# Conditioning matmuls in bursts of four tiles in the first mixer of a decoder step

## The chip, the cores and the metric

The kernel runs on one core of one Trainium2 chip. The metric is the device time of one execution, in microseconds, as the median of several runs. A core has five engines that run side by side, each through its own queue in program order: TensorE (matmuls, PE in the profile, with its weight loads as PEld), VectorE (DVE), ScalarE (ACT), GpSimd (POOL) and SyncE (SP). POOL and SP issue most of the transfers here.

## The reference

One inference step of two layers for 256 prompt tokens and 8 x 4 sample tokens, 288 columns, with a model width of 1024. Before each layer a conditioning vector `c` (9 of them: one for the prompt, eight for the samples) is turned into six sets of 1024 shifts, scales and gates:

```
mod = silu(c) @ w_ada[i] + b_ada[i]          # (9, 1024) @ (1024, 6144)
sh_m, sc_m, g_m, sh_f, sc_f, g_f = split(mod, 6)
hm  = x * (1 + sc_m) + sh_m
out = lru_mixer(hm, ...)                      # layer 0; a convolution mixer in layer 1
x   = layer_norm(ALPHA * x + g_m * out)
hf  = x * (1 + sc_f) + sh_f
x   = layer_norm(ALPHA * x + g_f * peer(hf))
```

The first mixer projects `hm` with `w_in` (1024 x 2560), runs a convolution over four positions, two gates and a recurrent scan on the first 1280 channels, multiplies by the gelu of the other 1280, and projects with `w_out` (1280 x 1024). `peer` picks 16 experts a head for each token by product keys. Shifts and scales of the mixer (`sh_m`, `sc_m`) are needed before it; `g_m`, `sh_f`, `sc_f` and `g_f` only behind it.

## The kernel before, in words

All activations lie transposed, channels on partitions. The program order of every engine is written out by hand: what stands first in the code comes first in that engine's queue.

*The first mixer* (`lru`). Two loops of ten. Step `h` of the first loop projects block `h` of the first half of `w_in` (`proj`, tile `prj`: 8 matmuls of 128 x 288 in f32, line 466, 16 instructions; blocks 6 to 9 are split into a high and a low part and take 24 quick matmuls, lines 457 to 459). ScalarE copies the result out (lines 755, 756, 676), VectorE runs the convolution (679, 680). In the same step come the gates of block `h - 2` (two matmuls into `pg`, line 692; ScalarE 693 to 696, VectorE 698 to 707) and, at step 9, two long root functions on ScalarE (715, 717) on which VectorE's scans (720 to 728) wait. The second loop projects the second half (ScalarE copy or gelu into `GG`, lines 778 and 780), with the scans and the products `yout` (742, high half `yH` 743 on ScalarE, low half `yL` 746 on VectorE) beside them. A projection's result lies in one of two PSUM buffers. Then `wout` multiplies by `w_out` (tile `po`), ten blocks of `yH` and `yL` for each of eight outputs.

*The conditioning* (`ada`). While the mixer runs, the other two thirds of layer 0's `mod` are computed: 32 tiles of `w_ada` (128 x 2 x 512, 512 KB each) in four parts of eight. `ada` is a generator; each step of it issues the load of the tile four ahead (POOL's queue, line 381, into a ring of six buffers that also holds the copies `adas`) and the two matmuls of one tile (tile `adap`, line 396; 4 instructions in the profile). The stationary operand has 32 columns, so a tile's output takes 32 of the 128 PSUM partitions and one 32-column strip of the array; the tiles of a row of four go to strips 0, 1, 2, 3, and the next four add to the same strips:

```
nc.tensor.matmul(pt[32 * q:32 * q + 32], self.cS[:, 2 * kp + kk, :], w[:, kk],
                 start=st and kk == 0, stop=sp and kk == 1,
                 skip_group_check=True)
```

The eighth tile of a part is followed by ScalarE's copy (403) in the same step; then comes one step that does nothing, and the step after that starts with four transposes (tile `adat`, line 415), VectorE's additions to `mod` (420), and the first tile of the next part. How many steps run after the projection of step `h` stands in two lists:

```
XA = [2] * 10      # first loop:  self.fill(gen, XA[h])
GA = [2] * 10      # second loop: self.fill(gen, GA[h])
```

What is left after the second loop is run at once (`run_all(gen)`).

*Weights* come as raw blocks over SP's queue into four buffers (line 213); blocks that are to be split are split by ScalarE (229) and VectorE (230).

Of the kernel before, what the change touches and what calls it, by code (L numbers as in the profile page):

```python
# [86 lines left out]
PM = 0  # L87
VO = (0, 2, 4, 6, 1, 3, 5, 7)
RH = 3
XA = [2] * 10  # L90
GA = [2] * 10
SLOW = 1.18
BG2 = 4
BG3 = (20, 24)
# [96 lines left out]
def interleave(gens):  # L191
    gens = list(gens)
    while gens:
        gens = [g for g in gens if next(g, "end") != "end"]
# [63 lines left out]
class Kern:  # L258
# [391 lines left out]
    def lru(self):  # L650
# [79 lines left out]
        def scan_s(h0):  # L730
            hh = slice(h0, h0 + 5)
            prev = fv("h0").rearrange("p (h b) -> p h b", b=NB)[:, hh]
            for s in range(NL):
                o = vs(tr)[:, hh, :, s]
                v.tensor_mul(o, vs(ti)[:, hh, :, s], prev)
                v.tensor_add(o, o, vs(XC)[:, hh, :, s])
                prev = o
            v.tensor_copy(hs[:, hh, 0], tr[:, hh, NP - 1])
            v.tensor_copy(hs[:, hh, 1:9], prev)

        def yout(h):
            v.tensor_mul(te[:, h], tr[:, h], GG[:, h])
            nc.scalar.copy(yH[:, h], te[:, h])
            yield
            yield
            v.tensor_sub(yL[:, h], te[:, h], yH[:, h].bitcast(F32))
# [4 lines left out]
        for h in range(HR):  # L751
# [15 lines left out]
            if SPLIT0 and S0 <= h < S0 + 4:  # L767
                for k in (2 * (h - S0), 2 * (h - S0) + 1):
                    self.split_act(self.aH[:, k], self.aL[:, k], hm[:, k])
            self.fill(gen, XA[h])  # L770
        lc = bp.tile([128, HR, 9, 3], F32, name="lc")
# [3 lines left out]
        for h in range(HR):  # L775
# [20 lines left out]
            for r in rs:  # L796
                if r in (4, 9):
                    scan_s(r - 4)
            self.fill(gen, GA[h])
        interleave([yout(h) for h in youts])  # L800
# [676 lines left out]
```

## Time and profile before

| what | value |
|---|---|
| runs | 2146.39 us median of 3 (2142.21, 2146.39, 2147.93) |
| profiled execution, first to last instruction (span) | 2144.5 us |
| profiled execution, time outside the span | not listed |
| TensorE busy | 2074.6 us, 97% |
| VectorE busy | 1763.2 us, 82% |
| ScalarE busy | 927.4 us, 43% |
| POOL busy | 213.1 us, 10% |
| mean granted TensorE clock | 0.988 of full speed |
| transfers | 460.30 MB, mean 215 GB/s |

The span counts from the first to the last instruction of one execution on the chip; busy is the time with at least one instruction on the engine. Matmuls are pipelined and their ends are modelled, so starts say more than ends. The first mixer's loops lie between 36 and 160 us of the span, the output projection `wout` between 160 and 192 us.

### The profile page before, as it was taken

What the parts mean: (1) busy time and instruction counts of PE and PEld (TensorE: products, weight loads), DVE (VectorE), ACT (ScalarE), POOL (GpSimd) and SP (SyncE); (2) the same over time, 40 slices, a digit from 0 to 9 for tenths busy, and PEclk for the clock granted to TensorE, in tenths of its full rate; (3) what the DMA queues carried; (4) which work ended last, traced back from release to release, by engine and by line L of the source; (5) the groups of instructions that cost most, each with busy time, mean ns of one, the idle gap of its engine ahead of it and who ended that gap; (6) DMA issues with size and microseconds to landing.
All of it is one profiled execution on the core that took longest, in us unless ns stands there. A gap on an engine that the chain in (4) does not pass through costs nothing.

```text
span 2144.5 us, 46937 instructions
## 1 busy us (share of the span) xinstructions
PE 2074.6 (97%) x19202; PEld 1924.8 (90%) x19202; DVE 1763.2 (82%) x3772; ACT 927.4 (43%) x1321; POOL 213.1 (10%) x249
## 2 busy tenths in 40 slices
PE   7999999999999999999988889999999999999997
PEld 3668899999999998999967569999999999999996
DVE  3686799799788998988777468998987989899886
ACT  1754444443444443444442454444434444444443
POOL 1100000000011222002112100000000111110120
PEclk9999999999999999999999899999999999999998
DMA  9656455555577777669759743655556777765793
GB/s 367 220 198 236 160 166 179 172 164 158 178 239 252 256 251 250 221 221 329 275 154 286 268 140 121 186 181 170 162 161 203 244 262 253 248 188 167 235 325 141
DMA packets 126184, 460.30 MB, mean 215 GB/s; under 512 B 14496, under 2 KB 15008, under 8 KB 125328
## 3 DMA queue, kind: packets, MB, share of 16 engines
q1 hardware_dynamic: 93168, 334.08, 48.1%
q0 software_dynamic: 32800, 123.22, 17.3%
q8 instruction: 150, 2.46, 0.5%
q14 instruction: 66, 0.54, 0.1%
HBM read 449.85 MB, written 7.39 MB: 213 GB/s over the span
## 4 chain that ended last, share of the span: by engine, by line
PE 90%; DVE 4%; DMA 3%; ACT 1%; issue 1%; POOL 0%; SPq 0%; ACTq 0%; DVEq 0%; POOLq 0%
PE acc L1286 12%; PE pu L457 11%; PE acc L1287 11%; PE pu L458 11%; PE acc L1288 11%; PE pu L459 11%; PE prj L466 3%; PE adap L396 3%; PE prj L457 2%; PE prj L459 2%; PE prj L458 2%; PE pgt L1231 2%; PE pgt L1233 2%; DMA R<-us 1%; PE pd L873 1%
## 5 line engine op out<-in xcount | busy, mean ns | idle before, releaser
L229 ACT CAST wh<-raw 128x1024 fp32r<-128x1024 f32 x583 | 611.4, 1050 | 632.8 <-PE acc L1287 384.4
L230 DVE TENSOR_TENSOR wl<-raw,wh 128x1024 fp32r<-128x1024 f32 x583 | 710.8, 1224 | 146.4 <-ACT wh L229 139.5
L1286 PE MATMUL acc<-gh,wh 128*128 128x256 f32 x2048 | 582.6, 284 | 2.0 <-ACT gh L433 2.0
L457 PE MATMUL pu<-aH,wh 128*128 128x256 f32 x2048 | 582.8, 285 | 0.0
L458 PE MATMUL pu<-aL,wh 128*128 128x256 f32 x2048 | 578.6, 283 | 0.2 <-issue 0.2
L459 PE MATMUL pu<-aH,wl 128*128 128x256 f32 x2048 | 575.0, 281 | 0.0
L1287 PE MATMUL acc<-gl,wh 128*128 128x256 f32 x2048 | 573.5, 280 | 0.6 <-DVE gl L434 0.5
L1288 PE MATMUL acc<-gh,wl 128*128 128x256 f32 x2048 | 572.6, 280 | 0.0
L457 PEld LDWEIGHTS pu<-aH,wh 128*128 128x128 f32 x2048 | 387.7, 189 | 1.0 <-issue 1.0
L1286 PEld LDWEIGHTS acc<-gh,wh 128*128 128x128 f32 x2048 | 385.4, 188 | 2.4 <-ACT gh L433 2.4
L458 PEld LDWEIGHTS pu<-aL,wh 128*128 128x128 f32 x2048 | 386.7, 189 | 0.4 <-issue 0.4
L1287 PEld LDWEIGHTS acc<-gl,wh 128*128 128x128 f32 x2048 | 384.9, 188 | 1.2 <-DVE gl L434 1.2
L459 PEld LDWEIGHTS pu<-aH,wl 128*128 128x128 f32 x2048 | 385.0, 188 | 0.0
L1288 PEld LDWEIGHTS acc<-gh,wl 128*128 128x128 f32 x2048 | 385.0, 188 | 0.0
L1249 DVE SCALAR_TENSOR_TENSOR store<-pgt,store 128x460 f32<-128x460 f32 (+6 forms) x184 | 170.3, 952 | 52.3 <-PE pgt L1233 48.7
L1308 ACT ACTIVATE store<-pu 128x512 f32<-128x512 f32 x128 | 76.7, 600 | 264.0 <-PE pu L459 264.0
L1366 POOL DMA_INDIRECT grow<-ur,ei x64 | 72.5, 1134 | 1059.5 <-DVE ei L1348 765.4
L1212 DVE TENSOR_TENSOR oA<-c,iT 128x1024 f16<-128x1024 f16 x192 | 132.1, 688 | 0.0
L434 DVE TENSOR_TENSOR gl<-store,gh 128x256 fp32r<-128x256 f32 x256 | 107.9, 422 | 15.4 <-ACT gh L433 15.1
L457 PE MATMUL prj<-aH,wh 128*128 128x288 f32 x392 | 120.1, 306 | 0.0
L459 PE MATMUL prj<-aH,wl 128*128 128x288 f32 x392 | 116.0, 296 | 0.2 <-DVE wl L230 0.2
L458 PE MATMUL prj<-aL,wh 128*128 128x288 f32 x392 | 116.1, 296 | 0.0
(346 smaller groups left out, 2632.0 us busy)
## 6 DMA issues: line engine op xcount, KB each, us to landing
raw<-ut SPq DMA_DIRECT2D x256, 512.0 KB
raw<-vt SPq DMA_DIRECT2D x256, 512.0 KB
adaw<-wada POOLq DMA_DIRECT2D x56, 512.0 KB
raw<-w SPq DMA_DIRECT2D x54, 512.0 KB
raw<-wq SPq DMA_DIRECT2D x32, 512.0 KB
adaw<-wada SPq DMA_DIRECT2D x18, 512.0 KB
R<-us POOLq DMA_DIRECT2D x32, 286.5 KB
store<-wada POOLq DMA_DIRECT2D x12, 512.0 KB
```

Of the source, the lines that this page charges most:

```text
L229: nc.scalar.copy(hf, r)
L230: nc.vector.tensor_sub(lf, r, hf.bitcast(F32))
L434: self.nc.vector.tensor_sub(lo, src, h.bitcast(F32))
L457: nc.tensor.matmul(pt, h[:, kb], ah[:, ka, n0:n1], start=f, stop=False)
L458: nc.tensor.matmul(pt, h[:, kb], al[:, ka, n0:n1], start=False, stop=False)
L459: nc.tensor.matmul(pt, lo[:, kb], ah[:, ka, n0:n1], start=False, stop=e)
L1212: v.tensor_tensor(a, self.iota2[:, None].to_broadcast([128, g, 128, 2]), bc(0, 128), op=ALU.is_equal)
L1249: v.scalar_tensor_tensor(sv, pg[:, :n, q0 - j0:q1 - j0], 1.0 / 4096.0, sv, op0=ALU.mult, op1=ALU.mult)
L1286: nc.tensor.matmul(o, vh[:, d], wh, start=f, stop=False, skip_group_check=True)
L1287: nc.tensor.matmul(o, vh[:, d], wl, start=False, stop=False, skip_group_check=True)
L1288: nc.tensor.matmul(o, vl[:, d], wh, start=False, stop=e, skip_group_check=True)
L1308: nc.scalar.activation(store[:, s:s + 2], pu, AF.Gelu)
```

## The change

Only the two lists change. After the projections 0 and 2 (and 5 and 7) of either loop four steps of the conditioning run, after 1, 3, 6 and 8 none, after 4 and 9 one. Both lists now have 18 steps, 36 together; what follows the 36th step, the last part's transposes and additions, runs behind the second loop.

```diff
-XA = [2] * 10
-GA = [2] * 10
+XA = [4, 0, 4, 0, 1] * 2
+GA = [4, 0, 4, 0, 1] * 2
```

## Rows read from the trace of the kernel before

**Rows 1.** Page, the chain that ended last: shares of the span by engine.

```profile
PE 90%; DVE 4%; DMA 3%; ACT 1%; issue 1%; POOL 0%; SPq 0%; ACTq 0%; DVEq 0%; POOLq 0%
```

**Rows 2.** Windows, both loops: stretch, us; PE, PEld, DVE, ACT, POOL; clock, DMA, GB/s.

```profile
36.00:100.00 64.00, 63.93 (x291) 41.13 (x292) 41.37 (x119) 35.20 (x84) 7.93 (x15) 0.97 0.77 276
100.00:160.00 60.00, 60.00 (x254) 36.36 (x253) 43.61 (x125) 34.59 (x56) 7.48 (x15) 1.00 0.58 191
```

**Rows 3.** The chain by time: start us, us on the chain, what.

```profile
41.91 1.85 PE adap L396 x8
43.76 4.08 PE prj L466 x16
...
53.76 0.97 PE pg L692 x4
...
68.52 0.44 PE adat L415 x4
```

**Rows 4.** Timeline of TensorE: start us, us, instructions merged.

```profile
41.84 1.92 PE L396 MATMUL adap<-adaw,cS 128*32 128x512 f32 x8
...
94.38 1.90 PE L396 MATMUL adap<-adaw,cS 128*32 128x512 f32 x4
...
160.23 0.29 PE L457 MATMUL po<-yH,wh 128*128 128x288 f32 x1
...
160.62 0.29 PE L457 MATMUL po<-yH,wh 128*128 128x288 f32 x1
...
198.88 3.68 PE L396 MATMUL adap<-ab,cS 128*32 128x512 f32 x32
```

**Rows 5.** Groups by line from 36.07 to 160.65 us: count, busy us, mean ns.

```profile
L396 PE MATMUL adap<-adaw,cS 128*32 128x512 f32 x128 | 34.5, 598 | 0.0
```

**Rows 6.** Timeline of POOL: when loads of tiles are issued.

```profile
34.96 0.53 POOL L381 DMA_DIRECT2D adaw<-wada  x1 [1.05 <-issue]
44.04 1.06 POOL L381 DMA_DIRECT2D adaw<-wada  x2 [8.55 <-PE adap L396]
...
77.97 1.05 POOL L381 DMA_DIRECT2D adaw<-wada  x2 [6.35 <-PE adap L396]
...
90.38 0.53 POOL L381 DMA_DIRECT2D adaw<-wada  x1 [5.15 <-PE adap L396]
```

**Rows 7.** Transfers: input; POOL's queue to 41.9, 47.4, 51.4; in 77.9:83.5, 90.3:94.1.

```profile
x<-xT POOLq DMA_DIRECT2D x1, 1152.0 KB
...
q0 software_dynamic: 721, 3.30, 21.0%
...
q0 software_dynamic: 1010, 4.35, 24.1%
...
q0 software_dynamic: 1301, 5.40, 27.7%
...
q0 software_dynamic: 288, 1.05, 49.3%
...
q0 software_dynamic: 144, 0.52, 46.5%
```

**Rows 8.** Windows: projection 6 of the first loop; roots to the last low half.

```profile
75.77:81.98 6.21, 6.21 (x37) 4.27 (x37) 4.96 (x12) 4.67 (x12) 1.05 (x2) 1.00 0.98 348
107.50:162.30 54.80, 54.80 (x238) 33.88 (x238) 44.26 (x126) 28.50 (x51) 4.78 (x9) 1.00 0.57 192
```

**Rows 9.** Timelines of ScalarE and VectorE: root function, first scan, last block.

```profile
105.59 1.88 ACT L717 ACTIVATE T<-T 128x2016 f32<-128x2016 f32 x1
...
107.50 0.46 DVE L720 TENSOR_TENSOR T<-T,T 128x288 f32<-128x288 f32 x1 [6.16 <-ACT T L717]
...
160.42 0.41 ACT L780 ACTIVATE GG<-prj 128x288 f32<-128x288 f32 x1 [1.32 <-PE prj L459]
...
161.83 0.46 DVE L746 TENSOR_TENSOR yL<-T,yH 128x288 fp32r<-128x288 f32 x1 [0.50 <-ACT yH L743]
```

**Rows 10.** Windows, columns as in rows 2: the first projection.

```profile
36.07:41.84 5.77, 5.77 (x16) 4.03 (x17) 3.17 (x13) 0.00 (x0) 0.00 (x0) 0.70 1.02 407
```

## The prediction

> **What bounds the kernel now.** I read the chain of waits first: TensorE holds 90% of it [rows 1]. Then the windows of the first mixer's two projection loops: TensorE is busy 63.93 of 64.00 us and 60.00 of 60.00 us there, while VectorE has 41.37 and 43.61 us of work, ScalarE 35.20 and 34.59 us [rows 2]. So in this stage every microsecond that leaves TensorE's queue leaves the path, as long as nobody else becomes late. The chain by time shows the pattern: a projection of 4.08 us, the gates 0.97 us, a burst of conditioning matmuls 1.85 us, and at four places 0.44 us of transposes [rows 3]. Nothing lies between the pieces.
>
> What a burst costs hardly depends on its tiles. Two tiles (8 instructions, on two column strips) take 1.92 us, one tile (4 instructions on one strip) 1.90 us, and eight tiles in a row, later in the kernel, 3.68 us [rows 4]. Four instructions of one strip go one behind the other; different strips go side by side. A burst costs what its fullest strip costs, about 1.85 us on the path.
>
> **The change, part by part.** *Bursts.* A part of the conditioning is eight tiles, then one empty step before its transposes. In steps of two, the 32 tiles of the four parts fall into 18 bursts: 14 of two tiles and 4 of one (14 x 8 + 4 x 4 = 128 instructions, which is the count of the row, 34.5 us) [rows 5]. With 4, 0, 4, 0, 1 they fall into 8 bursts of four tiles, each tile on its own strip: at projections 0, 2, 5, 7 of either loop. The single steps at 4 and 9 are the empty ones. No matmul is added or removed. A burst of four is not in the trace by itself. Its bounds: 1.84 us (half of the eight-tile row, which is two such groups; less it can't be, since one strip alone needs about that) and 3.70 us (only two strips at once). I take 1.85, by the eight-tile row [rows 4]. Ten bursts go: 10 x 1.85 = 18.5 us less on TensorE.
>
> The Trainium skill ("TensorE: Matmul & The Clock Gate", section "Measured speedup vs the span model") has four tiles packed side by side at 3.07 times the rate of one, not four. By that a burst of four would cost 4 x 1.90 / 3.07 = 2.48 us, an estimate, and the sum would lose 5.0 us of its 18.5. The trace does not agree: eight tiles one by one would be 15.2 us and took 3.68, which is 4.1 times.
>
> *The transposes* (four times 0.44 us), the ScalarE copies and the VectorE additions stay as many. The last transposes move from projection 8 of the second loop to behind it; 0.44 us on the path at either place.
>
> *Loads on POOL's queue.* Each tile's step issues the load of the tile four ahead, into one of six buffers; so loads bunch too. Tiles 6 to 9 wait only for the first burst and are then issued at once; later a burst releases three or four. POOL needs 1.05 us to issue two, and starts about 0.35 us after the burst that frees the buffers [rows 6, 3]. Behind waiting loads POOL has only the two output copies, for which nobody waits. The tile that arrives last in each burst decides:
> - First burst, at 41.84 us: all four tiles are now wanted at once, the third and fourth formerly one projection and burst later. POOL's queue carried the input (1152 KB, 1.18 MB) and four tiles of 0.524 MB, 3.28 MB, and had started 3.30 MB by 41.9 us [rows 7]. The fourth strip starts some 0.3 us late: 0.3 us lost.
> - Second burst, at about 52.8 us (41.84 + 1.85 + two projections + gates): the eighth tile makes 5.37 MB, and 5.40 MB had been started by 51.4 us [rows 7]. It waits behind the same tiles as before. Nothing lost, with a margin of 1.4 us.
> - The tight ones are projection 7 of either loop, 8.2 to 8.6 us after the burst of projection 5 (8.16 us is two projections of 4.08; in the first loop two split ones of some 3.3 us, which is 6.21 less 1.85 and 0.97, and two gates) [rows 3, 8]. Three tiles must land in it. One took 3.8 us from its issue, two 5.6 us beside the weight loads [rows 6, 7]; so a third lands after some 7.5 us, 7.9 with POOL's start. It fits by 0.3 to 0.7 us; both ends are 0 and 2 us a burst. I take 0.5 us for the two together.
>
> *VectorE and ScalarE.* In the first loop they fit on the whole: a plain stretch (projection and burst, 6.21 us) has 4.96 us of VectorE work and 4.67 of ScalarE [rows 8]; without a burst TensorE needs 4.4 us, so VectorE falls behind by 0.6 us there, and catches up at the next burst. TensorE asks for a projection's result only two projections later, so this costs nothing. Of ten bursts that go, five lie before the last projection of the first loop ends: ScalarE's long root functions there, which end at 107.47 us and let VectorE begin [rows 9], come 5 x 1.85 = 9.25 us earlier. From that point VectorE has 44.26 us of work in the 54.80 us until the last low half of the mixer's output is ready [rows 8, 9]. Shifted, that is 98.25 + 44.26 = 142.5 us without any wait, and about 146 with those that can't go (in the last link, ScalarE's gelu, product, high half and low half, 160.42 to 162.29 us, 1.9 us one behind the other [rows 9], and the copies and splits of weights before it). TensorE wants that half at the tenth block of the output projection, nine blocks of 0.39 us after its start at 160.23 us [rows 4]: at 163.8 us now and at 145.3 then. So VectorE becomes the bound by a little: TensorE waits 0 to 3 us, I take 0.7 us. Behind this waiting matmul the whole output projection stands. It is the one new wait.
>
> *After it.* The output projection and all later stages are fed by buffers that refill at their own pace, and TensorE leads there too [rows 1]; I carry the shift to the end, one for one.
>
> Sum: 18.5 - 0.3 - 0.5 - 0.7 = 17.0 us. The profiled execution's span is 2144.5 us; no time around it is listed for it, and the median of the runs is 2146.39 (2142.21 to 2147.93), 1.9 us above. Span after: 2127.5; time: 2146.4 - 17.0 = 2129.4 us.
>
> **The rivals.**
> - *VectorE holds the second loop.* Its waits in this stretch (54.80 - 44.26 = 10.5 us) are not TensorE's doing but its own order with ScalarE, and don't shrink. Then the output projection comes only 9.25 us earlier: 2137.1 us. For it: the stretch is 81% busy. Against: some of the waits end on projections (the gelu needs one), and these come earlier.
> - *Two strips at a time.* A burst of four costs 3.70 us: 8 x 3.70 = 29.6 us against 33.3, a gain of 3.7 us: 2142.7 us, no change. Against: eight tiles in 3.68 us.
> - *Strips overlap in part.* Halfway between the bounds, 2.77 us a burst, it is 33.3 - 8 x 2.77 = 11.1, less 0.8 for loads (VectorE is then in time): 10.3 us, 2136.1. The same row speaks against it. The page's rate above lies in this case; by it, 18.5 - 5.0 - 0.8 = 12.7 us, 2133.7.
> - *The gain is returned later:* a later stage waits for a load that comes when it came before. 2141 to 2148 us. Against: no load later on is without a buffer that TensorE frees.
> - *Slower: the bunched loads come late.* Place: the second burst and projections 7, 2 and 7 after it, each with two or three tiles asked for only when the burst before ended. At the start of this stage the transfers run at a DMA share of 1.02 and 407 GB/s [rows 10], and the sixth tile, issued at 34.96 us [rows 6], was in only at about 47.4 us, when POOL's queue had started the 4.33 MB of the input and six tiles [rows 7]: 12.4 us. If the bunches always queue so, each of four bursts waits 12.4 - 8.2 = 4.2 us, and TensorE falls to its lower clock: the stretch after the idle start has a granted 0.70 and 5.77 us for a projection of 4.08, 1.7 us more [rows 10]. 4 x 5.9 = 23.6 us against 18.5: slower by 5.1, 2151.5 us; below a wait of 2.9 us a burst it isn't slower. Against: from 77.97 us two tiles and the weights ran at 5.6 us for both, so such a queue is not the rule.
>
> **How the numbers follow.** My forecast (a gain of 13 to 20 us) 0.71; VectorE's hold 0.11; strips in part 0.04; two strips 0.04; returned later 0.05; late loads 0.05. A measurement of this kernel tells 0.3%, 6.4 us, from no change. Faster by more than that: forecast, VectorE's hold and strips in part, and a sliver of late loads that only cost part: 0.87. Same 0.09, slower 0.04. The range: 2124 (the full 18.5 us with 4 us of the runs' own scatter) to 2139 (VectorE's hold with 2 us on it).
>
> **What would show it.** Eight bursts of 16 instructions, each 1.85 to 2.0 us, at projections 0, 2, 5, 7 of both loops; TensorE without gaps through both loops; the output projection beginning at about 142 instead of 160.23 us, with a wait for VectorE's last low half of about 0.7 us near its tenth block; the rest of the trace the same, 17 us earlier. Wrong if: bursts of four take over 2.5 us; TensorE waits over 1 us for a tile at projection 7; the wait for the low half exceeds 3 us; or the shift at the output projection is not the shift at the end.

## The result, and the profile after

The changed kernel takes 2131.03 us (median of 6 runs, 2123.40 to 2133.94), the kernel before 2145.41 us in the same set (6 runs, 2142.21 to 2149.25): a ratio of 0.993, 95% interval 0.9913 to 0.9947. A second set of runs, on another occasion, gave 2130.23 us (2127.14 to 2131.16) against 2148.33: 0.9917, interval 0.9904 to 0.9931. The forecast was 2129.4 us, with a range of 2124 to 2139. The profiled execution of the changed kernel took 2130.04 us, with a span of 2128.3; that of before has 2144.5.

The page after: the span, and the chain's shares by engine, as in [rows 1].

```profile
span 2128.3 us, 46940 instructions
...
PE 86%; DVE 6%; DMA 4%; ACT 2%; issue 1%; POOL 0%; SPq 0%; ACTq 0%; DVEq 0%; POOLq 0%
```

TensorE's share of the chain went from 90 to 86%: other engines now hold some of the path. To see what changed in the first mixer, it is cut at four starts that can be found in either trace: its first projection, the second loop's first projection, the output projection, and the mean behind it. Windows of the kernel before (columns as in [rows 2]):

```profile
36.07:102.85 66.78, 66.78 (x304) 42.21 (x304) 41.95 (x120) 38.03 (x88) 9.03 (x18) 0.97 0.73 264
102.85:160.23 57.38, 57.38 (x243) 35.52 (x242) 43.19 (x123) 31.77 (x51) 6.38 (x12) 1.00 0.61 202
160.23:192.21 31.98, 31.98 (x242) 31.98 (x241) 21.08 (x46) 12.52 (x13) 0.00 (x0) 1.00 0.93 349
```

The same windows of the kernel after, and below them its first projection alone, which answers to [rows 10]:

```profile
36.84:92.25 55.41, 54.74 (x293) 39.34 (x293) 39.82 (x117) 35.37 (x85) 7.70 (x15) 1.00 0.83 308
92.25:142.27 50.02, 49.63 (x253) 35.00 (x252) 40.82 (x118) 31.97 (x51) 7.89 (x16) 1.00 0.68 229
142.27:175.87 33.60, 33.08 (x243) 32.25 (x242) 24.29 (x55) 14.04 (x16) 0.00 (x0) 1.00 0.93 351
36.84:41.12 4.28, 4.28 (x16) 2.70 (x16) 3.16 (x13) 0.00 (x0) 0.00 (x0) 1.00 1.03 410
```

The first loop is 11.4 us shorter, the second 7.4, the output projection 1.6 us longer; together 17.1. TensorE, which was busy in every microsecond of these stretches, now has small gaps in each. They can be seen in its timeline (kernel after, columns as in [rows 4]; what ended an idle time stands in brackets):

```profile
41.12 1.93 PE L396 MATMUL adap<-adaw,cS 128*32 128x512 f32 x12
43.73 1.90 PE L396 MATMUL adap<-adaw,cS 128*32 128x512 f32 x4 [0.67 <-DMA adaw<-wada]
45.56 8.03 PE L466 MATMUL prj<-hm,raw 128*128 128x288 f32 x32
53.42 1.13 PE L692 MATMUL pg<-XC,wg 128*128 128x288 f32 x4
54.49 1.94 PE L396 MATMUL adap<-adaw,cS 128*32 128x512 f32 x16
56.36 4.15 PE L466 MATMUL prj<-hm,raw 128*128 128x288 f32 x16
60.34 1.13 PE L692 MATMUL pg<-XC,wg 128*128 128x288 f32 x4
61.31 4.04 PE L466 MATMUL prj<-hm,raw 128*128 128x288 f32 x16
65.19 1.13 PE L692 MATMUL pg<-XC,wg 128*128 128x288 f32 x4
...
81.95 1.94 PE L396 MATMUL adap<-adaw,cS 128*32 128x512 f32 x16
...
132.41 1.94 PE L396 MATMUL adap<-adaw,cS 128*32 128x512 f32 x16
134.75 4.15 PE L466 MATMUL prj<-hm,raw 128*128 128x288 f32 x16 [0.39 <-ACT GG L780]
...
142.27 0.38 PE L457 MATMUL po<-yH,wh 128*128 128x288 f32 x1
...
147.01 0.40 PE L457 MATMUL po<-yH,wh 128*128 128x288 f32 x1 [0.43 <-ACT yH L743]
```

Three things are to be seen. Bursts of four tiles (x16) take 1.94 us, where two tiles took 1.92 [rows 4]; there are seven such, and the first burst, which comes in two pieces: three strips at 41.12, the fourth at 43.73, when its tile is there, and it takes its own 1.90 us. The other bursts, those at projection 7 included (81.95 and 132.41), wait for no tile. And TensorE now waits for ScalarE's `GG` once and, at the output projection, for the last block of `yH` and `yL`. The last transposes come at 141.92, ahead of the output projection; it begins at 142.27 where the forecast had about 142. From the mean on (175.87 against 192.21) the kernel after is 16.3 us earlier, which is the 17.1 us less the 0.8 us by which its first projection starts later; at the end of the span it is 16.2 us: the shift is carried. One pair of traces shows that only to within some us, for what stands behind the mean took 1952.3 us before, and 1952.4 and 1949.0 us in two profiles of the changed kernel.

### The profile page after: what moved, and what is told of

It reads as the page before. It is cut to its first block, busy times and chain, and to the rows that moved or that the text cites. A ratio compares the mean times of both kernels' runs of the same rounds, so it can differ in the third digit from the quotient of the medians.

```text
span 2128.3 us, 46940 instructions
## 1 busy us (share of the span) xinstructions
PE 2055.1 (97%) x19202; PEld 1922.0 (90%) x19202; DVE 1761.3 (83%) x3772; ACT 926.6 (44%) x1321; POOL 219.6 (10%) x249
## 4 chain that ended last, share of the span: by engine, by line
PE 86%; DVE 6%; DMA 4%; ACT 2%; issue 1%; POOL 0%; SPq 0%; ACTq 0%; DVEq 0%; POOLq 0%
PE acc L1286 12%; PE pu L457 11%; PE acc L1287 11%; PE pu L458 11%; PE acc L1288 11%; PE pu L459 11%; PE prj L457 2%; PE pgt L1231 2%; PE prj L459 2%; PE prj L458 2%; PE pgt L1233 2%; PE adap L396 2%; DMA R<-us 2%; PE prj L466 1%; DMA us<-UB 1%
## 5 line engine op out<-in xcount | busy, mean ns | idle before, releaser
L1366 POOL DMA_INDIRECT grow<-ur,ei x64 | 77.0, 1204 | 1054.5 <-DVE ei L1348 766.5
```

Of the source, the lines that this page charges most:

```text
L1366: nc.gpsimd.indirect_dma_start(out=r, out_offset=None, in_=tab, in_offset=bass.IndirectOffsetOnAxis(ap=ei[:, w, c:c + 1], axis=0))
```

## The experiments

The marker in most of them is the time from the first projection of the mixer to the mean behind its output projection (156.14 us before, 139.03 after), or from the second loop's first projection to the mean (89.36 before, 83.62 after). It is steadier than the time of the whole execution: the second profile of the changed kernel has 138.98 and 83.62. The longer marker holds the first projection, which takes some 1.5 us more when its granted clock is 0.70 and not 1.00, so that clock is given where it matters.

**The first burst one projection later.**

```diff
-XA = [4, 0, 4, 0, 1] * 2
+XA = [0, 4, 0, 4, 1, 4, 0, 4, 0, 1]
```

> The changed kernel with the first two bursts one projection later (steps 0, 4, 0, 4, 1 in the first five places); as many bursts of four. The stretch from the first projection's start to the mean's first matmul is 139.0 us in the changed kernel. Theory: its first burst takes 4.44 us because the fourth tile has not landed (three strips at 41.12, the fourth strip alone at 43.73); later by a projection all four are there: 1.9 us a burst everywhere, the stretch 136.4 us. Rival: a first burst of four has its own cost after the one-strip stretch before it; the burst stays above 4 us and the stretch at 139 us. If the second burst, now after projection 3, waits for tiles instead, the stretch stays at 138 to 139 us.

One run, 2132.82 us; marker 140.11. The first burst is whole (1.94 us), but the gain is gone elsewhere: its first projection ran at a granted clock of 0.70 (5.67 us), and at projection 7 a tile came late. Timeline of TensorE:

```profile
80.01 1.93 PE L396 MATMUL adap<-adaw,cS 128*32 128x512 f32 x12
82.20 1.90 PE L396 MATMUL adap<-adaw,cS 128*32 128x512 f32 x4 [0.26 <-DMA adaw<-wada]
```

The burst ends 82.20 - 80.01 = 2.2 us later than a whole one, not 0.26: a strip that starts late ends late by as much, and the idle time in brackets shows only what the other three strips don't cover. So the time between the bursts of projections 5 and 7 (71.48 to 80.01, 8.5 us, the same as in the kernel after) is about what three loads need, now enough and now not. As a repair it missed: 136.4 us were expected.

**Two strips at a time.** The same work, but every burst in the mixer holds two tiles of one strip and then two of the next.

```diff
-             for i, r in enumerate(o):
-                 jobs += [(l, b, k0, k1, q, kp, g, i == 0, i == len(o) - 1) for q, (kp, g) in enumerate(r)]
+             rows = [[(l, b, k0, k1, q, kp, g, i == 0, i == len(o) - 1) for q, (kp, g) in enumerate(r)]
+                     for i, r in enumerate(o)]
+             if l == 0 and b:
+                 rows = [[r[q] for r in rows] for q in range(4)]
+             for r in rows:
+                 jobs += r
```

> The changed kernel with the tiles of a part in another order: a burst of four now fills two strips twice (0, 0, 1, 1 and 2, 2, 3, 3) and not four strips once. The number of bursts, tiles and loads is the same. Theory (strips side by side): eight rounds of 0.43 us a burst, 3.5 us, so 8 x 1.7 us more; about 2 us of VectorE's waits and 1.8 us of the first burst's wait go, so the stretch from first projection to mean is 147 to 151 us (139.0 changed, 156.1 before) and the whole 9 to 11 us slower than the changed kernel. Rival (the gain comes from fewer changes between bursts and projections, each with a fixed cost): bursts of about 1.9 us, the stretch 137 to 140 us, no difference in the whole.

2156.41 us in three rounds, ratio 1.0027 (1.0012 to 1.0042) to the kernel before; marker 161.90. Each burst:

```profile
54.97 5.37 PE L400 MATMUL adap<-adaw,cS 128*32 128x512 f32 x16
```

The same 16 instructions take 5.37 us where four strips take 1.94; 3.5 us and a marker of 147 to 151 us were expected, so the direction was right and the size missed. The single starts show why it is more than the 3.7 us of two strips in turn: the matmuls begin every 0.43 us, the first tile alone (54.97, 55.42, 55.85, 56.28), then the second beside the third (56.71 and 56.715), then the fourth alone: twelve beats of 0.43. In the kernel after the four strips start 13 ns apart (54.486, 54.500, 54.513, 54.526) and go four beats. With as few bursts as the changed kernel the gain is gone, so it is the strips and not the number of bursts; and the order inside a burst decides: here a tile overlapped with the next one in the queue only where that one was for another strip.

**One loop alone.**

```diff
-GA = [4, 0, 4, 0, 1] * 2
+GA = [2] * 10
```

> The new step list in the first loop alone; the second loop keeps two steps at each projection. 13 bursts instead of 18 or 8. Theory: each burst that goes is worth 2.07 us (1.87 of its own and 0.2 at the start of the next projection), and the first burst loses 2.6 us: the stretch from first projection to mean is 156.1 - 10.4 + 2.6 = 148.4 us, 1.5 us less if the first projection runs at the full clock; no wait for VectorE's low half at the output projection. Rival (each burst is worth its 1.85 alone): 149.5 us.

```diff
-XA = [4, 0, 4, 0, 1] * 2
+XA = [2] * 9 + [0]
```

> The new step list in the second loop alone; the first loop keeps two steps at each projection (the tenth has none). 13 bursts. Theory: VectorE's chain from the root functions to the last low half starts when it started before and needs about 48 us, so TensorE waits for it at the output projection: 5 x 2.07 = 10.4 us go, 3 to 4 us come back as waits; the stretch from first projection to mean is 149 to 150 us (1.5 us less if the first projection runs at the full clock). Rival (VectorE holds nothing): 145.8 us, no wait over 0.5 us at the output projection.

First loop alone: 2142.19 us (one run), marker 149.84. Second loop alone: 2137.80 (one run), marker 147.82. Either gives part of the 17.1 us, and both missed: the first had its first projection at full clock, for which 146.9 us were expected, the second at 0.71, for which 149 to 150 were. The first falls short mostly by two rows of TensorE's timeline that the kernel after doesn't have so: an even later fourth tile in the first burst, and transposes that wait 1.75 us for ScalarE's copy. An empty step still stands before these; but the copy now lies in ScalarE's queue behind table loads and long functions (lines 715, 717 and 789), which run from 117.47 us on, and starts at 124.06. In the kernel before, the same copy starts at 122.69, ahead of them, and nobody waits.

```profile
40.97 2.35 PE L396 MATMUL adap<-adaw,cS 128*32 128x512 f32 x12
44.29 1.90 PE L396 MATMUL adap<-adaw,cS 128*32 128x512 f32 x4 [0.97 <-DMA adaw<-wada]
...
124.68 0.66 PE L415 MATMUL adat<-c,adas 128*128 128x128 f32 x4 [1.75 <-ACT adas L403]
```

The second, whose waits were expected at 3 to 4 us, says where the one of 1.6 us at the output projection comes from. With bursts of four in the second loop alone its stretch from output projection to mean is 33.58 us, as in the kernel after (33.60); with them in the first loop alone it is 32.08, as before (31.98). The wait goes with the shorter second loop.

**The last low halves on GpSimd.** Takes nine of ten low halves `yL` from VectorE; the second time with the spread schedule below.

```diff
+YV = (9,)
...
-             v.tensor_sub(yL[:, h], te[:, h], yH[:, h].bitcast(F32))
+             (v if h in YV else nc.gpsimd).tensor_sub(yL[:, h], te[:, h], yH[:, h].bitcast(F32))
```

> The changed kernel with nine of the ten low halves of the mixer's output taken by GpSimd instead of VectorE: 9 x 0.37 = 3.3 us less in VectorE's chain of 47.9 us from the root functions to the last low half. Theory (VectorE's chain is late for the output projection): the 0.4 us wait before projection 8 and the 1.6 us at the output projection shrink, the stretch from first projection to mean goes from 139.0 to 137.0 us (1.5 us more if the first projection runs at the lower clock). Rival 1 (the chain is ScalarE's, or the hand-overs between the two): 139 us as before. Rival 2 (GpSimd is slower at it, or the two slow each other): the last low halves come later, over 139.5 us.

> The two former ones together: bursts at projections 1, 3, 5, 8 in the first loop, and nine low halves on GpSimd. If the late fourth tile and VectorE's chain are separate losses: 139.0 - 2.6 - 2.0 = 134.4 us from first projection to mean (135.9 at the lower clock of the first projection). If they are one loss: 136.4 us or more.

2139.17 and 2136.24 us (one run each), markers of the second loop 93.84 and 93.52: slower, for a reason of its own. POOL's queue also issues the tiles' loads, and these now stand behind low halves that wait for ScalarE. Timelines of POOL and of TensorE in the first of the two:

```profile
127.97 2.85 POOL L747 TENSOR_TENSOR yL<-T,yH 128x288 fp32r<-128x288 f32 x1 [16.07 <-ACT yH L744]
134.49 1.54 POOL L747 TENSOR_TENSOR yL<-T,yH 128x288 fp32r<-128x288 f32 x2 [3.68 <-ACT yH L744]
135.97 2.13 POOL L382 DMA_DIRECT2D adaw<-wada  x4
```

```profile
140.36 6.40 PE L397 MATMUL adap<-adaw,cS 128*32 128x512 f32 x16 [7.68 <-DMA adaw<-wada]
```

The four loads leave at 135.97 and TensorE stands 7.68 us. So neither run answers whether VectorE's load matters.

**Bursts spread over the first loop.**

```diff
-XA = [4, 0, 4, 0, 1] * 2
+XA = [0, 4, 0, 4, 1, 4, 0, 0, 4, 1]
```

> The changed kernel with the first loop's bursts at projections 1, 3, 5 and 8 (steps 0, 4, 0, 4, 1, 4, 0, 0, 4, 1): as many bursts, each at least one projection later or further from the one before, so that the fourth tile has landed. Theory (a late fourth tile repeats the whole four rounds, 1.9 us, on top of the wait): all bursts 1.9 us, no wait for a tile, the stretch from first projection to mean 136.4 us at the full clock of the first projection, 137.9 at the lower. Rival (what TensorE wins in the first loop VectorE gives back in the second): 139 us.

> The kernel with the first loop's bursts at projections 1, 3, 5, 8, timed. Theory: 2.6 us below the changed kernel in the first loop and nothing in the second, so a ratio to the kernel before of 0.991 to 0.992; rival (the late fourth tile is rare): 0.993, as the changed kernel.

2127.67 us (one run), then 2127.49 (2123.15 to 2131.15) in five rounds: ratio 0.9907 (0.9892 to 0.9923), beside 0.9917 for the kernel after in the same set; the intervals overlap. The markers are 137.49 and 136.22, where 137.9 and 136.4 were expected. All eight bursts are whole (1.94 us) and no tile is waited for. The two markers differ by the clock of the first projection: the second ran at full clock, the first did not.

**Bursts of half the work in the second loop.** The second 128 rows of each tile are left out in the second loop. This takes four times 0.87 us from TensorE there, and nothing from the other engines.

```diff
-             for kk in range(2):
+             kn = 1 if l == 0 and b == 2 else 2
+             for kk in range(kn):
```

> The changed kernel with half the conditioning matmuls of the second loop left out (the second 128 rows of each tile of the last two parts): bursts there of two rounds, about 1.0 instead of 1.87 us, 3.4 us less on TensorE. Theory (VectorE's chain of 47.9 us from the root functions sets the end of the second loop): the output projection begins up to 3.4 us earlier and waits as much longer for the last low half; the stretch from first projection to mean stays within 0.7 us of 139.0 (1.5 us more at the lower clock of the first projection). Rival (TensorE still leads there): 135.6 us.

2134.89 us (one run). In the second loop four bursts take 1.07 us instead of 1.94, which takes 3.4 us from TensorE, and its marker does not move: 83.67 us against 83.62. The time came back as waits of TensorE for ScalarE's `GG`:

```profile
119.64 4.15 PE L467 MATMUL prj<-hm,raw 128*128 128x288 f32 x16 [0.32 <-ACT GG L781]
...
126.64 8.31 PE L467 MATMUL prj<-hm,raw 128*128 128x288 f32 x32 [1.43 <-ACT GG L781]
...
137.53 4.15 PE L467 MATMUL prj<-hm,raw 128*128 128x288 f32 x16 [1.59 <-ACT GG L781]
```

The wait was expected at the output projection and came earlier, but its sum is 3.3 us. So with bursts of four the second loop's end is no longer TensorE's. (The whole time is longer than after's by the first burst, whose fourth tile came 4.8 us late in this run; that loop's work is unchanged.)

**Is it VectorE's load?** The spread schedule, with the low halves of blocks 3 to 8 on GpSimd, at a place where no load is left to be held up.

```diff
+YV = (0, 1, 2, 9)
...
+             (v if h in YV else nc.gpsimd).tensor_sub(yL[:, h], te[:, h], yH[:, h].bitcast(F32))
```

> First loop's bursts at projections 1, 3, 5, 8; GpSimd takes only the low halves 3 to 8, which stand behind the last tile load in its queue, so no load waits for them. VectorE loses 6 x 0.37 = 2.2 us of its chain of 47.9. Theory (that chain sets the end of the second loop): the stretch from the second loop's first projection to the mean, 83.4 to 83.7 us in every run with four bursts there, falls to 81.5 to 82.2 us; the whole 4 us below the changed kernel, 20 us below the one before. Rival (ScalarE or the hand-overs set the chain): 83.4 us or more.

2130.77 us (2127.51 to 2141.53), ratio 0.9931 (0.9911 to 0.9952). The marker is 83.70: VectorE was relieved of six low halves and the end did not come earlier. The expectation of 81.5 to 82.2 us failed. TensorE still waited for the same half, and once for a weight's low part besides:

```profile
143.89 0.40 PE L460 MATMUL po<-yH,wl 128*128 128x288 f32 x1 [0.17 <-DVE wl L231]
144.72 0.40 PE L458 MATMUL po<-yH,wh 128*128 128x288 f32 x1 [0.43 <-ACT yH L744]
```

VectorE's own rows say where the relief went. Its splits of weights waited 0.49, 0.97 and 0.47 us for ScalarE in the kernel after; here they waited:

```profile
134.95 1.37 DVE L231 TENSOR_TENSOR wl<-raw,wh 128x1024 fp32r<-128x1024 f32 x1 [1.45 <-ACT wh L230]
...
138.99 1.23 DVE L231 TENSOR_TENSOR wl<-raw,wh 128x1024 fp32r<-128x1024 f32 x1 [1.93 <-ACT wh L230]
...
142.43 1.41 DVE L231 TENSOR_TENSOR wl<-raw,wh 128x1024 fp32r<-128x1024 f32 x1 [1.47 <-ACT wh L230]
```

All six halves lie in the last 14 us of the chain that ends with the last low half. So the run says nothing on VectorE's work ahead of these, and there it is full: in the kernel after it is busy 26.42 of the 26.90 us from 106.67 to 133.57.

**Or the hand-overs?** The chain by time at the end of the second loop shows how ScalarE and VectorE take turns (kernel after; pieces under 0.05 us are left out):

```profile
142.69 0.38 DVE T L742
143.15 0.77 ACT yH L743 x2
143.92 0.96 ACT wh L229
144.90 1.23 DVE wl L230
146.13 0.38 DVE T L742
146.53 0.44 ACT yH L743
146.99 0.47 DVE yL L746
147.51 0.40 PE po L458
```

A product, its high half, then the split of a weight block (0.96 us on ScalarE and 1.23 on VectorE, one behind the other), then the next product: from 133.57 to 147.45 neither engine is full (VectorE 10.88 us of 13.88, ScalarE 8.65), but each waits for the other. The last run has the spread schedule and takes one split out of the chain; weight block 19 is multiplied as it is, with 16 slow instructions instead of 24 quick ones.

```diff
-SPLIT0 = (6,7,8,9,19)
+SPLIT0 = (6, 7, 8, 9)
```

> The schedule of e6_bursts_spread, but weight block 19 (the last of the second loop) is left as raw f32: its split into a high and a low part goes from ScalarE and VectorE, and the last projection runs as 16 slow instructions instead of 24 quick ones (TensorE +0.7 us). Marker: from the first projection of the second loop to the mean's matmul behind the output projection, 83.36 us in e6_timed, of which TensorE's work is some 81.5. Theory A (the hand-overs between ScalarE and VectorE in the second loop set its end, and the split casts stand among them): the chain from the first scan to the last low half, 47.9 us in all runs so far, falls by 1.0 to 2.2 us, TensorE's wait in the output projection falls below 0.7 us, marker 82.0 to 82.7 (TensorE then sets the end, with the 0.7 us on it). Theory B (the chain doesn't run through the splits): chain 47.9 unchanged or later by the longer last projection, marker 83.4 to 84.1. The time moves by less than 1 us in either case.

2124.96 us (2123.29 to 2125.61), ratio 0.9890 (0.9874 to 0.9907). Second loop's marker 82.56 against 83.36, though TensorE has 0.7 us more to do in it. VectorE's first scan and last low half in the spread schedule, with split:

```profile
96.11 0.46 DVE L720 TENSOR_TENSOR T<-T,T 128x288 f32<-128x288 f32 x1 [6.16 <-ACT T L717]
...
143.57 0.46 DVE L746 TENSOR_TENSOR yL<-T,yH 128x288 fp32r<-128x288 f32 x1 [0.50 <-ACT yH L743]
```

and without:

```profile
96.42 0.46 DVE L720 TENSOR_TENSOR T<-T,T 128x288 f32<-128x288 f32 x1 [6.17 <-ACT T L717]
...
142.18 0.46 DVE L746 TENSOR_TENSOR yL<-T,yH 128x288 fp32r<-128x288 f32 x1 [0.50 <-ACT yH L743]
```

From 47.9 to 46.2 us: the chain is 1.7 us shorter, the output projection takes 32.07 us to the mean and waits no more. The 1.7 us are more than the split's 0.96 us on ScalarE, and less work for VectorE alone brought nothing, so in the last 14 us the turns of both set the pace, with the splits among them. Whether less work for VectorE ahead of these turns would bring the end forward, no run tried. This kernel and the spread one before it have lower medians than the kernel after; the intervals overlap, so only the markers tell the three apart (135.40 and 136.22 with the first projection at full clock; 139.03 for the kernel after, at full clock too).

## Why the prediction was right

The mechanism was right: a burst costs what its fullest strip costs, so ten bursts fewer take their time off TensorE's queue and off the path. That the sum of 17.0 us and the marker's 17.1 agree so closely is luck, for single terms were off on both sides and cancel; the medians of the whole time differ by 14.4 us in the first set and by 18.1 in the second. Where a burst's tiles are late the loss is read as the late strip's start less the burst's.

| term | forecast, us | measured, us |
|---|---|---|
| ten bursts fewer | 18.5 | 20.2 |
| first burst, late fourth tile | -0.3 | -2.6 |
| two bursts at projection 7 | -0.5 | 0 |
| TensorE waits for `GG` | 0 | -0.4 |
| wait at the output projection | -0.7 | -1.6 |
| first projection at full clock | 0 | +1.5 |
| sum | 17.0 | 17.1 |

*Bursts.* The shorter loops less the first projection and burst (59.16 to 46.69, 57.38 to 50.03) with the 0.39 us wait put back are 20.2 us for ten bursts, 2.02 each. The rows of the timeline after show it: the burst itself is 1.87 (54.49 to 56.36), but the gates ahead of it last 1.07 to its start and 0.97 where a projection follows (53.42, 60.34), and the projection behind it 3.98 against 3.88 (56.36, 61.31). The two changes between full-width and strip matmuls cost 0.1 us each, and go with the burst. The chain had put them to the neighbours [rows 3]. The Trainium skill ("TensorEngine Tiling (Array Packing)", section "Key Properties") says that a change of tiling mode drains TensorE, without a price. These rows agree with it; that the 0.1 us is the drain is not shown.

*Four strips side by side* was right: 1.94 us, inside 1.85 to 2.0. The two rivals of slower strips fall by the same row. The 3.07 of the Trainium skill ("TensorE: Matmul & The Clock Gate", section "Measured speedup vs the span model") is its row for four tiles packed by rows. Four packed by columns do better here: 4 x 1.90 / 1.94 = 3.9.

*The first burst* was mis-sized most, 2.6 us for 0.3. Taken by its whole length (41.12 to 45.56, 4.4 us) it also meets the sign "bursts of four take over 2.5 us", though its strips were not slow. The prediction set the tile against the moment when the queue had started its bytes. In the trace after, the queue's packets, counted in the order of their starts, make up the input and four tiles by 42.49 us, and the matmul is released only at 43.73; the chain shows it as one piece up to 43.68:

```profile
32.87 10.81 DMA adaw<-wada
43.68 0.04 issue
```

So 1.2 us from that count to the release were left out. The count was reached 0.35 us later than taken, and the burst wanted the tile 0.72 us earlier (41.12 for 41.84), since the first projection ran at full clock: 0.3 + 0.35 + 1.24 + 0.72 = 2.6. The trace has more on the 1.2 us: a tile's landing is told by sixteen signals, and this tile's come one by one from 42.35 to 43.68 us. In the half-burst run the same count is reached at 42.49 us too, and fifteen signals are in by 43.77, but the last comes at 44.78 and the strip starts at 44.82. So a matmul waits for the last of sixteen parts, and that part's lateness is not in the queue's bytes. The Trainium skill ("DMA: Bandwidth & Descriptors", section "Anatomy of one DMA — SWDGE (gpsimd) path") puts most of a transfer's fixed 2 us behind its last byte. How much of the 1.2 us lies behind the tile's last byte, and how much is a part that ran late, no run here shows.

The first clock is not the change's doing: granted 1.00 here, 0.70 before [rows 10], and 0.70 in the second profile of the changed kernel. There the first projection takes 5.77 us, the tile is only 1.0 us late, and the loop takes 55.36 us against 55.41: what the clock gives, the tile takes back.

*Projection 7* cost nothing, inside its bounds of 0 to 2; the first experiment, with 2.2 us there, shows how thin that is.

*The output projection's wait* was foreseen in its place, and its 1.6 us lie in 0 to 3. VectorE's chain from its first scan to the last low half was right as well: 47.8 us by the forecast (98.25 to about 146), 47.9 measured (99.52 to 147.45), of which 43.54 are work. What was off is its start: the scans began 8.0 us earlier than before and not 9.25, with the late first burst ahead of them. The forecast named waits that can't go, and the experiments show what they are: the turns of ScalarE and VectorE in the last 14 us, which don't shrink with TensorE's queue. The rival of a VectorE that holds the second loop had such waits too, but said that all 10.5 us of them stay; 4.4 us stayed (47.93 less 43.54), and the hold is 2.0 us and not 9.25. Of these 2.0 the 0.4 us for `GG` were not foreseen.

*Returned later* fell: 16.3 us at the mean, 16.2 at the end, and both sets of runs are faster by 14 us or more. The slower rival fell too: its four places wait for no tile in the kernel after. Its price, though, was shown at a fifth place, the first burst, and at projection 7 in one experiment.

## What to carry to other kernels

Matmuls of 32 columns on four strips cost what one strip costs if neighbours in the queue are for different strips (0, 1, 2, 3), so gather them before counting instructions; the two changes of width are saved as well. For a tile that gates a burst, count to its release and not to the queue's bytes, and look at the strip that starts last: the idle time shown before it is less than it costs. When an engine at 100% gets relief, look next at the chain of the engine that feeds it: its sum of work, and on top of it the turns with a third engine that won't shrink (43.5 and 4.4 us here).

## What was not expected of the hardware

The same four tiles in the order 0, 0, 1, 1 took 5.37 us, 2.8 times that of 0, 1, 2, 3, and more than two by two would (3.70): the second tile of a strip holds up the other strips' tiles behind it. And after a wait TensorE can be at the lower of its clock's two levels, 1.2 GHz of 2.4. Windows of the half-burst run: first projection, three strips, and, after an idle time of 1.96 us, the late fourth strip, which took 3.48 us instead of 1.90.

```profile
35.71:40.01 4.30, 4.30 (x17) 2.72 (x17) 3.17 (x13) 0.00 (x0) 0.00 (x0) 1.00 1.03 411
40.01:42.86 2.85, 2.85 (x13) 0.70 (x12) 1.76 (x6) 0.95 (x3) 0.65 (x2) 1.00 1.04 415
44.82:48.23 3.41, 3.41 (x4) 0.48 (x4) 0.00 (x0) 0.00 (x0) 0.00 (x0) 0.53 1.02 408
```

A late tile can so cost twice, by its wait and by the clock behind it (0.53 granted here, 1.00 in the kernel after, where the idle time was 0.67 us). That the wait brought the lower clock is not shown: the first projections, after 1.65 or 1.66 us of idle time in every run, had 0.70 in some and 1.00 in others.
